# Two more pairs of gates as seven-product jobs, and the gated branch woven into the attention

## The chip, the cores and the metric

The kernel runs on one core of a Trainium2 chip. The metric is the device time of one execution in microseconds. The core has a matrix engine (TensorE, PE in the profile), a vector engine (VectorE, DVE), a scalar engine (ScalarE, ACT), GpSimd (POOL) and SyncE (SP), which here only issues DMAs. Each engine takes its instructions in the order in which they stand in its own list, and waits where an operand or a buffer is not ready.

## The reference

One decoder layer over 1024 tokens with 1024 channels, in float32. What matters here is its first half:

```python
xn = rms_norm(h, norm_mix_g)
sb_q, sb_k, sb_v, g_q, g_k, g_v, g_r, g_a, gate_sb, gate_gla = split(xn @ w_in)
o_sb = stick_breaking_attention(sb_q, sb_k, sb_v)       # 8 heads of 64, strictly causal
log_a = log_sigmoid(g_a @ w_alpha_up + b_alpha) / 16
o_gla = gla_chunked(g_q * 64 ** -0.5, g_k, g_v, log_a)  # 4 heads, gated linear attention
o_gla = o_gla * rsqrt(mean(o_gla ** 2) + eps) * gla_norm_g * silu(g_r)
y = sigmoid(gate_sb + b_gate[0]) * (o_sb @ w_branch_sb) + sigmoid(gate_gla + b_gate[1]) * (o_gla @ w_branch_gla)
h = h + y @ w_out
```

In the stick-breaking attention the weight of token s for token t is `sigmoid(z) * prod(sigmoid(-z))` over the tokens between them. A feed-forward part with a causal convolution and a last norm follow; the change doesn't touch them.

## The kernel before

Each large product is made of two-part numbers: `split` (line 119) makes a high part with a ScalarE cast and the rest with a VectorE subtraction, and `mac` (196) multiplies high by high, high by low and low by high. A matmul has 128 x 128 weights and up to 512 columns.

The stages, in the program's order:

1. Norm and turning of x, then the values of the attention (`value`, line 367) and of the gated branch. Beside the latter, `sums` makes four sums of the quarters of x (VectorE), and `differences` the difference of each value row from the one before (SP loads, one POOL subtraction on line 445, a POOL store to `dv_d`).
2. Jobs (`fast`): two columns of 128 of `w_in` are multiplied by x with seven quarter products in place of eight, 7 x 12 = 84 matmuls a job. `project_pairs` lists them: queries, keys, the gated branch's swish gates, and the first `N_GATES` = 4 of the 16 merge gates, 10 pairs in all. `decayed` runs beside them as `side`.
3. `attend`: 8 heads, 8 rows of 128 tokens, 288 blocks of 128 x 128. A piece of up to four blocks goes through scores (664), a sigmoid (666), a POOL select that sets what lies over the diagonal to 1 (668), a scan along the row that multiplies from the diagonal leftwards (671), transposes (678), `split`, and `gather` with the value differences (687). `gather` evicts the lower half with a bias (692), adds the upper half (116) and stores to `osb_d` (695). Up to six pieces or 12 blocks (`AHEAD`, `BLOCKS`) lie between the scan and the transposes.
4. `gates` computes the other 12 gates directly, 48 matmuls a gate, in steps of six matmuls of 512 columns. It is a generator: the attention takes one step of it for every `FILL` = 3.6 blocks, a few more at its start, and `BEFORE` = 4 follow it. These steps fill PE between the attention's short matmuls.
5. `gated` (states 781, scores 805, outputs 818 and 830, root mean square 842 to 847, transposes 853) comes behind, woven at two to three with `first_branch`, the product of the attention's output with `w_branch_sb`. This needs `osb_d` loaded back and split (955, 956).
6. The second branch, the output product, the feed-forward part.

Tiles come from pools: `t2` holds 11 of 128 x 512, `t4` 14 of twice that, `t8` 16 of four times; a tile is given out anew when its last reader is done. A scheduler puts the instructions of these generators in order for each engine.

Of the kernel before, what the change touches and what calls it, by code (L numbers as in the profile page):

```python
# [65 lines left out]
def block_kernel(ctx: ExitStack, tc: tile.TileContext, x, norm_mix_g, w_in, b_gate, w_alpha_up, b_alpha,  # L66
# [368 lines left out]
    def differences(i):  # L435

        a, b = t2(), t2()
        rows = slice(i * P, (i + 1) * P)
# [6 lines left out]
        nc.gpsimd.tensor_tensor(out=a, in0=a, in1=b, op=ALU.subtract)
# [211 lines left out]
    def weigh(t, e, i, b0, b1, right):  # L657
# [8 lines left out]
        nc.scalar.activation(ke[:, 0:w], z[:, 0:w], AF.Sigmoid, scale=-SBD ** -0.5)  # L666
        if right is None:
            nc.gpsimd.affine_select(out=ke[:, w - P:w], in_=ke[:, w - P:w], pattern=[[-1, P]],  # L668
                                    compare_op=ALU.is_gt, fill=1.0, base=0, channel_multiplier=1)
# [1 line left out]
        nc.vector.tensor_tensor_scan(out=kr, data0=kr, data1=zero.to_broadcast([P, w]),  # L671
                                     initial=1.0 if right is None else right[:, 0:1], op0=ALU.mult, op1=ALU.add)
# [8 lines left out]
    def gather(head, tp, ah, al):  # L681
# [7 lines left out]
        o = by(t2(), 2)  # L689
        for n in range(2):  # L690
            c = slice(n * P, (n + 1) * P)
            nc.scalar.activation(o[0:64, 1, c], po[64:128, c], AF.Identity,
                                 bias=vend[:, head * NT + 2 * tp + n:head * NT + 2 * tp + n + 1])
# [1 line left out]
        nc.sync.dma_start(osb_d[head * 64:(head + 1) * 64, tp * 2 * P:(tp + 1) * 2 * P], o[0:64, 0])
# [52 lines left out]
    owed = 0  # L748
    for w in attend():
        owed += w + EACH  # L750
        while owed >= FILL:
            owed -= FILL
            fill(gate_steps, 1)

# [6 lines left out]
    small = [by(t2(), 4) for _ in range(2)]  # L761
    state = [(v[:, 0], v[:, 1]) for v in small]

    gv, gla = [], []
    for p in range(2):
        rows = slice(p * P, (p + 1) * P)
        v, kt = by(t8(F32), 2), t4()
        nc.sync.dma_start(kt, kt_d[rows, :])
        v4 = by(t8(F32), 4)
        nc.sync.dma_start(v4, gv_d[p * HALF:(p + 1) * HALF, :].rearrange("(n p) c -> p n c", p=P))  # L770
        gv += [v4[:, n] for n in range(4)]
        nc.sync.dma_start(v[:, 0], qd_d[rows, :])
        nc.sync.dma_start(v[:, 1], ki_d[rows, :])
        gla.append((v[:, 0], v[:, 1], by(kt, NT), by(t4(), NT)))
# [103 lines left out]


# [69 lines left out]
    fill(gate_steps, BEFORE)  # L949
    ob = []  # L950
    for th in range(2):
        ob.append(quarter())
        for k in range(4):
            raw = t2()
            nc.sync.dma_start(raw, osb_d[k * P:(k + 1) * P, th * HALF:(th + 1) * HALF])
# [326 lines left out]
```

## Time and profile before

| | |
|---|---|
| median of 3 runs | 1410.92 us (1410.8 to 1413.48) |
| the profiled execution | 1412.8 us |
| its span | 1411.1 us |
| mean granted clock of TensorE | 0.994 |

The time is that of the whole execution, the span runs from the first to the last recorded instruction. In a view by stretches each row gives for one stretch the busy time of each engine with its number of instructions, then the granted TensorE clock as a share of full speed, and the DMA's share and rate. A chain of waits is read in order of time: each piece is what the next one waited for. Groups give the busy time, the mean of one instruction in ns, and the idle time of the engine before them. A matmul of float32 numbers that are not split stands there as two records.

### The profile page before, as it was taken

Reading aid. Unit: us, or ns where it says so; the run is one execution under the profiler, and the core shown is the slowest. Engines: PE = TensorE matmul, PEld = TensorE weight load, DVE = VectorE, ACT = ScalarE, POOL = GpSimd, SP = SyncE. Lnnn points to the kernel's source line nnn. Section 1 sums busy time; section 2 is a strip of 40 time slices with the busy share of each in tenths; the row PEclk is TensorE's granted clock in tenths of the full one; section 3 lists DMA queues with packets and bytes.
Section 4 is the critical chain, followed back from the end, with each engine's and each line's share of the span. In section 5 each row is a group of like instructions: output and inputs, shape, how many; then the busy total and the mean of one; then the engine's idle time right before and its main releaser. Section 6 shows DMA issues by size and latency. Waiting matters only on the chain.

```text
span 1411.1 us, 18434 instructions
## 1 busy us (share of the span) xinstructions
PE 1385.3 (98%) x6577; PEld 1145.4 (81%) x6577; DVE 1065.4 (76%) x1642; ACT 650.4 (46%) x1246; POOL 111.5 (8%) x198
## 2 busy tenths in 40 slices
PE   7999999999999999999999999999999999999997
PEld 6787888888888888878888788888888888888886
DVE  6398766767888875638446998998888977896765
ACT  6234444647766664543234543333333333454653
POOL 0040000001211110300000000100000000000000
PEclk9999999999999999999999999999999999999999
DMA  6365144276534346465324434564554437953332
GB/s 249 141 203 148 47 142 142 82 211 203 152 94 122 113 150 202 167 224 179 117 93 135 103 107 149 189 209 140 179 179 149 159 106 270 328 163 101 98 106 97
DMA packets 160188, 216.87 MB, mean 154 GB/s; under 512 B 10026, under 2 KB 103276, under 8 KB 159584
## 3 DMA queue, kind: packets, MB, share of 16 engines
q1 hardware_dynamic: 140848, 157.56, 36.5%
q0 software_dynamic: 11952, 43.58, 8.1%
q10 hardware_dynamic: 7296, 14.55, 2.8%
q8 instruction: 52, 0.85, 0.2%
q14 instruction: 40, 0.33, 0.1%
HBM read 155.75 MB, written 59.90 MB: 153 GB/s over the span
## 4 chain that ended last, share of the span: by engine, by line
PE 79%; issue 11%; DVE 6%; DMA 2%; ACT 1%; POOL 1%; POOLq 0%; ACTq 0%; DVEq 0%; SPq 0%
PE bank L196 46%; PE bank L1145 15%; PE bank L1012 5%; PE bank L367 3%; DVE t L110 3%; PE bank L687 2%; DVE t L116 2%; PE bank L664 2%; PE bank L678 2%; PE bank L320 1%; DMA gate_d<-t 1%; PE bank L427 1%; PE bank L818 1%; ACT t L119 0%; PE bank L781 0%
## 5 line engine op out<-in xcount | busy, mean ns | idle before, releaser
L196 PE MATMUL bank<-t,t 128*128 128x512 f32 x3648 | 870.6, 394 | 3.0 <-DVE t L110 2.6
L196 PEld LDWEIGHTS bank<-t,t 128*128 128x128 f32 x3648 | 682.7, 189 | 150.6 <-DVE t L110 3.8
L110 DVE TENSOR_TENSOR t<-t,t 128x512 fp32r<-128x512 f32 (+2 forms) x651 | 430.9, 696 | 82.6 <-ACT t L119 76.0
L119 ACT CAST t<-t 128x512 fp32r<-128x512 f32 x537 | 311.8, 620 | 321.5 <-DVE t L116 74.0
L116 DVE TENSOR_TENSOR t<-bank,t 128x512 f32<-128x512 f32 (+1 forms) x284 | 183.2, 655 | 119.9 <-PE bank L196 65.3
L1145 PE MATMUL bank<-t,t 128*128 128x512 f32 x924 | 209.6, 389 | 0.0
L1145 PEld LDWEIGHTS bank<-t,t 128*128 128x128 f32 x924 | 173.4, 188 | 36.0
L110 DVE TENSOR_TENSOR t<-t 128x512 f32<-128x512 f32 (+1 forms) x124 | 88.4, 721 | 5.6 <-DMA t<-in_w_ffn_in_dram 3.2
L367 PE MATMUL bank<-t,t 128*128 128x512 f32 x384 | 91.9, 398 | 0.0
L110 DVE TENSOR_TENSOR t<-bank,t 128x512 fp32r<-128x512 f32 (+4 forms) x128 | 72.2, 576 | 24.3 <-ACT t L119 23.9
L116 DVE TENSOR_TENSOR t<-t,t 128x512 f32<-128x512 f32 x107 | 76.8, 750 | 16.1 <-ACT t L487 15.4
L1012 PE MATMUL bank<-t,t 128*128 128x512 f32 x384 | 88.9, 391 | 0.0
L1043 ACT ACTIVATE t<-t,vcol 128x1024 f32<-128x1024 f32 x22 | 27.4, 1244 | 127.6 <-DVE t L116 124.0
L367 PEld LDWEIGHTS bank<-t,t 128*128 128x128 f32 x384 | 72.8, 192 | 15.6 <-DVE t L110 0.4
L1012 PEld LDWEIGHTS bank<-t,t 128*128 128x128 f32 x384 | 71.6, 188 | 14.7
L119 ACT CAST t<-bank 128x512 fp32r<-128x512 f32 (+3 forms) x124 | 61.6, 509 | 40.2 <-PE bank L320 19.7
L1045 DVE SCALAR_TENSOR_TENSOR t<-t,vcol,t 128x1023 f32<-128x1023 f32 (+1 forms) x44 | 56.3, 1279 | 14.1 <-ACT t L1043 13.9
L671 DVE TENSOR_TENSOR_SCAN t<-t,zero 128x128 f32<-128x128 f32 (+1 forms) x64 | 52.2, 823 | 16.0 <-POOL t L668 15.5
L664 PE MATMUL bank<-t,t 128*128 128x128 f32 (+3 forms) x192 | 55.5, 368 | 0.4 <-DVE t L110 0.4
L678 PE MATMUL bank<-ident,t 128*128 128x128 f32 x288 | 52.3, 274 | 0.8 <-DVE t L116 0.4
L668 POOL TENSOR_SCALAR_AFFINE_SELECT t<-t 128x128 f32<-128x128 f32 x64 | 33.3, 526 | 212.4 <-ACT t L666 199.2
L666 ACT ACTIVATE t<-bank 128x128 f32<-128x128 f32 (+3 forms) x96 | 45.7, 499 | 6.0 <-PE bank L664 4.3
(127 smaller groups left out, 773.6 us busy)
## 6 DMA issues: line engine op xcount, KB each, us to landing
t<-in_w_ffn_in_dram SPq DMA_DIRECT2D x50, 512.0 KB, 4.2
t<-in_w_in_dram SPq DMA_DIRECT2D x43, 512.0 KB, 5.3
act_d<-t POOLq DMA_DIRECT2D x22, 512.0 KB, 6.0
t<-in_w_ffn_out_dram SPq DMA_DIRECT2D x22, 512.0 KB, 7.5
wsum_d<-t POOLq DMA_DIRECT2D x22, 512.0 KB, 4.1
t<-act_d SPq DMA_DIRECT2D x22, 512.0 KB, 6.1
t<-wsum_d SPq DMA_DIRECT2D x44, 256.0 KB, 3.1
t<-sqk_d SPq DMA_DIRECT2D x40, 256.0 KB, 4.2
```

The costliest lines, as they stand in the source:

```text
L110: nc.vector.tensor_tensor(out=o, in0=a, in1=b, op=ALU.subtract)
L116: nc.vector.tensor_tensor(out=o, in0=a, in1=b, op=ALU.add)
L119: nc.scalar.copy(h, src)
L196: nc.tensor.matmul(pt, a[:, kk], b[:, kk], start=start and kk == 0 and m == 0, stop=stop and kk == k - 1 and m == 2)
L367: nc.tensor.matmul(pt, a[:, k % 4, t], b, start=k == 0 and m == 0, stop=k == NK - 1 and m == 2)
L664: nc.tensor.matmul(z[:, 0:w], q[:, a, e, ts_], kk[:, e, b0 * P:b1 * P], start=a == 0, stop=a == 1)
L666: nc.scalar.activation(ke[:, 0:w], z[:, 0:w], AF.Sigmoid, scale=-SBD ** -0.5)
L671: nc.vector.tensor_tensor_scan(out=kr, data0=kr, data1=zero.to_broadcast([P, w]), initial=1.0 if right is None else right[:, 0:1], op0=ALU ...
L678: nc.tensor.transpose(pt[:, b * P:(b + 1) * P], ke[:, b * P:(b + 1) * P], ident)
L1012: nc.tensor.matmul(pt, a[:, k % 4, t], b, start=(k == 0 and m == 0), stop=(k == NK - 1 and m == 2))
L1045: nc.vector.scalar_tensor_tensor(out=cv[:, i:], in0=av[:, :S - i], scalar=col(V_CW, (2 - i) * NF + f), in1=cv[:, i:], op0=ALU.mult, op1=AL ...
L1145: nc.tensor.matmul(pts[m][i], a[:, t], b, start=(k == 0 and x_ == 0), stop=(k == NH - 1 and x_ == 2))
```

## The change

`N_GATES` becomes 8: two more pairs of gates are jobs, 12 in all, and 8 gates are left to `gates`. `gates_and_gated` chains the remaining gate steps, the loads of the gated branch (`fetch_gated`) and the steps of `gated`, and the attention takes its filling from this chain; what is left of it behind the attention is woven with `first_branch`. `differences` leaves the stage of the sums, and is called from the loop over the jobs; its loads go from SP's queue to POOL's. The select is gone: a mask `above` that is made once enters the scan as second operand, with a maximum. `gather` stores both halves apart, and they are added behind the load of `osb_d`.

```diff
-N_GATES = 4
+N_GATES = 8
...
-        nc.sync.dma_start(b, sbv_d[rows, :])
+        nc.gpsimd.dma_start(b, sbv_d[rows, :])
...
     for i in range(NT):
-        differences(i)
         fill(xsums, 2)
         value(ws2, (i + 4) % NT, gv_d)
...
     for n, _ in enumerate(steps):
         if n > 0 and n % 2 == 0:
             fill(side, 1)
+        elif n // 2 < NT:
+            differences(n // 2)
...
+    above = t2()
+    nc.gpsimd.memset(above[:, P:], 0.0)
+    nc.gpsimd.memset(above[:, 0:P], 1.0)
+    nc.gpsimd.affine_select(out=above[:, 0:P], in_=above[:, 0:P], pattern=[[-1, P]], compare_op=ALU.is_ge, fill=0.0,
+                            base=P - 1, channel_multiplier=-1)
...
         if right is None:
-            nc.gpsimd.affine_select(out=ke[:, w - P:w], in_=ke[:, w - P:w], pattern=[[-1, P]],
-                                    compare_op=ALU.is_gt, fill=1.0, base=0, channel_multiplier=1)
-        kr = ke[:, 0:w][:, ::-1]
-        nc.vector.tensor_tensor_scan(out=kr, data0=kr, data1=zero.to_broadcast([P, w]),
-                                     initial=1.0 if right is None else right[:, 0:1], op0=ALU.mult, op1=ALU.add)
+            nc.vector.tensor_tensor_scan(out=kr, data0=kr, data1=above[:, 0:w], initial=1.0, op0=ALU.mult, op1=ALU.max)
+        else:
+            nc.vector.tensor_tensor_scan(out=kr, data0=kr, data1=zero.to_broadcast([P, w]), initial=right[:, 0:1],
+                                         op0=ALU.mult, op1=ALU.add)
...
-            nc.scalar.activation(o[0:64, 1, c], po[64:128, c], AF.Identity,
-                                 bias=vend[:, head * NT + 2 * tp + n:head * NT + 2 * tp + n + 1])
-        add(o[0:64, 0], po[0:64, 0:2 * P], o[0:64, 1])
-        nc.sync.dma_start(osb_d[head * 64:(head + 1) * 64, tp * 2 * P:(tp + 1) * 2 * P], o[0:64, 0])
+            nc.scalar.activation(o[:, c], po[:, c], AF.Identity, bias=vend[:, i:i + 1])
+        for n, r in enumerate(HALVES):
+            nc.sync.dma_start(osb_d[n * HALF + head * 64:n * HALF + (head + 1) * 64, tp * 2 * P:(tp + 1) * 2 * P], o[r])
...
+    def gates_and_gated():
+
+        yield from gate_steps
+        xq.clear()
+        fetch_gated()
+        yield
+        yield from gated()
+
+    filling = gates_and_gated()
+    owed = 0
+    for w in attend():
+        owed += w + EACH
+        while owed >= FILL:
+            owed -= FILL
+            fill(filling, 1)
...
-    fill(gate_steps, BEFORE)
+    fill(filling, BEFORE)
...
-            raw = t2()
-            nc.sync.dma_start(raw, osb_d[k * P:(k + 1) * P, th * HALF:(th + 1) * HALF])
-            split(*(a[:, k] for a in ob[th]), raw)
+            halves = t2(), t2()
+            for n, v in enumerate(halves):
+                nc.sync.dma_start(v, osb_d[n * HALF + k * P:n * HALF + (k + 1) * P, th * HALF:(th + 1) * HALF])
+            add(halves[0], *halves)
+            split(*(a[:, k] for a in ob[th]), halves[0])
     first_branch = branch(0, ob, w_branch_sb)
     fill(first_branch, 1)
-    fill(gate_steps, 128)
-    xq.clear()
-    og = [quarter() for _ in range(2)]
     n = 0
-    for _ in gated():
+    for _ in filling:
```

How this moves instructions is seen best at three places. In the rows below a name gives the tile that is written, behind the arrow the tiles that are read, and then the shape; the line is that of the kernel whose rows they are.

On PE in the last quarter of the attention, before: transposes (L678), scores (L664), and the matmuls of a direct gate (L196) between them.

```order
L678 MATMUL bank_5144<-ident,t_928_5030 128x128 x3
L664 MATMUL bank_5150<-t_794_4362,t_843_4627 128x384 x2
L196 MATMUL bank_5115<-t_485_2831,t_899_4915 128x512
L196 MATMUL bank_5115<-t_484_2830,t_899_4915 128x512 x2
L196 MATMUL bank_5115<-t_485_2831,t_899_4915 128x512
L196 MATMUL bank_5115<-t_484_2830,t_899_4915 128x512
L678 MATMUL bank_5171<-ident,t_934_5070 128x128 x4
L664 MATMUL bank_5178<-t_794_4362,t_843_4627 128x512 x2
L678 MATMUL bank_5190<-ident,t_937_5087 128x128 x4
L664 MATMUL bank_5197<-t_794_4362,t_843_4627 128x512 x2
```

And in the changed kernel, where L686 are the transposes, L672 the scores, L806 and L769 outputs and states of the gated branch:

```order
L686 MATMUL bank_5083<-ident,t_949_4966 128x128
L686 MATMUL bank_5087<-ident,t_951_4972 128x128 x4
L672 MATMUL bank_5094<-t_844_4523,t_904_4782 128x256 x2
L686 MATMUL bank_5100<-ident,t_955_4990 128x128 x2
L672 MATMUL bank_5105<-t_844_4523,t_904_4782 128x512 x2
L806 MATMUL bank_5111<-t_886_4728,t_964_5030 128x128 x4
L686 MATMUL bank_5121<-ident,t_961_5017 128x128 x4
L672 MATMUL bank_5128<-t_844_4523,t_904_4782 128x384 x2
L769 MATMUL bank_5134<-t_890_4736,t_885_4726 128x256
```

The gate's matmuls of 512 columns have gone from between the attention's, and one state or one output of four short matmuls stands in the place of each step.

On PE at the end of the attention, before, from the last gather (L687) on; the matmuls behind it are of two direct gates:

```order
L687 MATMUL bank_5322<-t_946_5125,t_526_3021 128x128
L196 MATMUL bank_5230<-t_55_321,t_953_5168 128x512 x2
L196 MATMUL bank_5230<-t_56_322,t_953_5168 128x512
L196 MATMUL bank_5230<-t_55_321,t_953_5168 128x512
L196 MATMUL bank_5373<-t_484_2830,t_966_5243 128x512
L196 MATMUL bank_5373<-t_485_2831,t_966_5243 128x512
L196 MATMUL bank_5373<-t_484_2830,t_966_5243 128x512 x2
L196 MATMUL bank_5373<-t_485_2831,t_966_5243 128x512
L196 MATMUL bank_5373<-t_484_2830,t_966_5243 128x512 x2
```

And now, from the last scores of an output pair (L793) behind the last gather on; L841 are its transposes:

```order
L793 MATMUL bank_5486<-t_884_4725 128x128
L841 MATMUL bank_5501<-ident,t_1050_5422 128x128 x4
L806 MATMUL bank_5509<-t_890_4736,t_1061_5495 128x128 x4
L841 MATMUL bank_5515<-ident,t_1053_5436 128x128 x4
L806 MATMUL bank_5510<-t_890_4736,t_1062_5498 128x128 x4
L818 MATMUL bank_5509<-t_887_4732,t_884_4725 128x128
L818 MATMUL bank_5510<-t_887_4732,t_884_4725 128x128
```

Behind the last gather there were 41 matmuls of gates ahead of the first one of `first_branch`; now there are 15 scores, 8 transposes and 16 output matmuls of the gated branch, and eight scores of the next pair.

On ACT, one output pair of the gated branch, before (squares L842, root L843, scaling L847), among casts of the branch's weights:

```order
L842 ACTIVATE t_1049_5659,ss_1050_5660<-bank_5613 128x128 x4
L842 ACTIVATE t_1052_5673,ss_1053_5674<-bank_5614 128x128
L843 ACT_TABLE_LOAD
L843 ACTIVATE ss_1050_5660<-ss_1050_5660,eps 128x4
L842 ACTIVATE t_1052_5673,ss_1053_5674<-bank_5614 128x128 x2
L847 ACTIVATE t_1049_5659<-bank_5613,ss_1050_5660 128x128 x4
L842 ACTIVATE t_1052_5673,ss_1053_5674<-bank_5614 128x128
L119 CAST t_1132_6149<-t_1131_6147 128x512
L843 ACTIVATE ss_1053_5674<-ss_1053_5674,eps 128x4
```

And now the first of them, which stands in the attention (squares L830, root L831, scaling L835, the attention's sigmoid L674):

```order
L830 ACTIVATE t_1007_5197,ss_1008_5198<-bank_5111 128x128 x4
L830 ACTIVATE t_1010_5211,ss_1011_5212<-bank_5112 128x128
L831 ACT_TABLE_LOAD
L831 ACTIVATE ss_1008_5198<-ss_1008_5198,eps 128x4
L830 ACTIVATE t_1010_5211,ss_1011_5212<-bank_5112 128x128 x2
L835 ACTIVATE t_1007_5197<-bank_5111,ss_1008_5198 128x128 x4
L830 ACTIVATE t_1010_5211,ss_1011_5212<-bank_5112 128x128
L119 CAST t_966_5036<-bank_5224 128x4x128
L831 ACTIVATE ss_1011_5212<-ss_1011_5212,eps 128x4
L674 ACT_TABLE_LOAD
L674 ACTIVATE t_1014_5234<-bank_5231 128x512
L835 ACTIVATE t_1010_5211<-bank_5112,ss_1011_5212 128x128 x4
```

The pair now has the attention's sigmoid behind it, and a second table load ahead of that one.

More of the change, by code (lines that the diff above doesn't have):

```diff
@@ L159, in block_kernel @@
     gate_d, ga_d = dram("gate_d", 2 * D, S), dram("ga_d", 2 * RANK, S)
-    osb_d = dram("osb_d", SBH * SBD, S)
+    osb_d = dram("osb_d", 2 * SBH * SBD, S)
     x21_d = dram("x21_d", 2 * P, 2 * D)
@@ L438, in differences @@
         rows = slice(i * P, (i + 1) * P)
-        nc.sync.dma_start(b, sbv_d[rows, :])
+        nc.gpsimd.dma_start(b, sbv_d[rows, :])
         if i == 0:
             nc.gpsimd.memset(a[0:1], 0.0)
-            nc.sync.dma_start(a[1:P], sbv_d[0:P - 1, :])
+            nc.gpsimd.dma_start(a[1:P], sbv_d[0:P - 1, :])
         else:
-            nc.sync.dma_start(a, sbv_d[i * P - 1:(i + 1) * P - 1, :])
+            nc.gpsimd.dma_start(a, sbv_d[i * P - 1:(i + 1) * P - 1, :])
         nc.gpsimd.tensor_tensor(out=a, in0=a, in1=b, op=ALU.subtract)
@@ L635, in block_kernel @@
     vt = []
-    vend = t2()[0:SBD, 0:SBH * NT]
+    vend = t2()[:, 0:SBH * NT]
+    above = t2()
[3 more added lines that the diff above has]
+                            base=P - 1, channel_multiplier=-1)
     def last_values():
@@ L644, in last_values @@
             nc.tensor.transpose(pt[0:SBD, h * NT:(h + 1) * NT], raw[0:NT, h * SBD:(h + 1) * SBD], ident[0:NT, 0:NT])
-        nc.vector.tensor_copy(vend, pt[0:SBD, 0:SBH * NT])
+        nc.gpsimd.memset(vend[SBD:P], 0.0)
+        nc.vector.tensor_copy(vend[0:SBD], pt[0:SBD, 0:SBH * NT])
     def value_blocks(n):
@@ L747, in block_kernel @@
     last_values()
[L748 to L753, printed above, removed]
     def after(b, a):
@@ L759, in after @@
                           reason="bank order")
[L761 to L774, printed above, removed]
+    state, gv, gla, og = [], [], [], []
     def states(p, n0, n1):
@@ L877, in gated, with fetch_gated @@
                     yield
+    def fetch_gated():
+        small = [by(t2(), 4) for _ in range(2)]
+        state.extend((v[:, 0], v[:, 1]) for v in small)
+        for p in range(2):
+            rows = slice(p * P, (p + 1) * P)
+            v, kt = by(t8(F32), 2), t4()
+            nc.sync.dma_start(kt, kt_d[rows, :])
+            v4 = by(t8(F32), 4)
+            nc.sync.dma_start(v4, gv_d[p * HALF:(p + 1) * HALF, :].rearrange("(n p) c -> p n c", p=P))
+            gv.extend(v4[:, n] for n in range(4))
+            nc.sync.dma_start(v[:, 0], qd_d[rows, :])
+            nc.sync.dma_start(v[:, 1], ki_d[rows, :])
+            gla.append((v[:, 0], v[:, 1], by(kt, NT), by(t4(), NT)))
+        og.extend(quarter() for _ in range(2))
+    def gates_and_gated():
[11 more added lines that the diff above has]
+            fill(filling, 1)
     yq, yb, hq, hs1 = {}, {}, {}, {}
```

4 lines of the change are left out of this document (3 added, 1 removed).

## The prediction

> **What bounds the kernel now.** I read the page's busy shares first, then busy time by stretches, then the chain of waits, and only then single instructions.
>
> ```profile
> span 1411.1 us, 18434 instructions
> PE 1385.3 (98%) x6577; PEld 1145.4 (81%) x6577; DVE 1065.4 (76%) x1642; ACT 650.4 (46%) x1246; POOL 111.5 (8%) x198
> ```
>
> TensorE is busy 98% of the span, so a gain must take matmuls away or fill one of the few places where PE waits. The stretches show where these are, and how near the second engine is.
>
> ```profile
> 105.00:140.00 35.00, 32.89 (x134) 25.30 (x133) 29.92 (x47) 13.97 (x25) 2.53 (x3) 0.95 0.50 149
> 455.00:490.00 35.00, 35.00 (x204) 30.17 (x203) 30.43 (x43) 21.51 (x47) 6.33 (x10) 1.00 0.39 114
> 560.00:595.00 35.00, 35.00 (x222) 28.80 (x221) 23.99 (x51) 20.50 (x70) 10.50 (x18) 1.00 0.61 205
> 595.00:630.00 35.00, 32.31 (x184) 25.90 (x183) 15.08 (x27) 16.96 (x68) 2.37 (x4) 0.90 0.58 197
> 665.00:700.00 35.00, 35.00 (x157) 28.96 (x156) 19.13 (x31) 7.69 (x13) 0.00 (x0) 1.00 0.22 68
> ```
>
> Columns after the length: PE, PEld, DVE, ACT, POOL, granted clock, DMA. Two stretches lose time: 105 to 140 (2.11 us idle, and a clock of 0.95 costs about 1.75) and 595 to 630 (2.69 idle, clock 0.90, about 3.5). In the attention (455 to 490) PE is full, but VectorE already works 30.4 of 35 us. That nearness decides this change: the attention has matmuls of the gates woven in, which cost PE much and VectorE little.
>
> **Matmuls removed.** Four gates leave the direct form (96 matmuls a pair) for jobs of 84, so 2 x 12 = 24 matmuls of 512 columns go.
>
> ```profile
> 795.95 396.51 PE bank L196 x1748
> ```
>
> One takes 396.51 / 1748 = 0.2268 us back to back: 24 x 0.2268 = **-5.4 us**, all of it on PE, which bounds there. The jobs add VectorE and ScalarE work, but in their stretch VectorE has room; I price that at nothing.
>
> **The differences leave the sums.** At 70 to 117 VectorE makes the sums of x, and the chain of waits runs through it until PE gets its operand:
>
> ```profile
> 115.88 0.61 DVE t L110
> 116.54 3.73 PE bank L196 x10
> ```
>
> ```profile
> 74.83 2.38 DVE L116 TENSOR_TENSOR t<-t,t 128x512 f32<-128x512 f32 x2
> 83.22 1.28 DVE L116 TENSOR_TENSOR t<-t,t 128x512 f32<-128x512 f32 x2
> ```
>
> ```profile
> 75.14 1.52 POOL L445 TENSOR_TENSOR t<-t,t 128x512 f32<-128x512 f32 x1 [20.36 <-DMA t<-sbv_d]
> ```
>
> A pair of adds takes 1.28 us alone and 2.38 us where a POOL subtraction runs beside it: 1.1 us. Eight such subtractions are in that stretch; 8 x 1.1 = 8.8 us is more than PE waits for. They move to the jobs, nine of them now since block 0 is done twice, with their loads on POOL's queue instead of SP's. What they hold up there is POOL's own stores behind them, and VectorE, which has room.
>
> ```profile
> 112.00:117.00 5.00, 3.23 (x15) 2.37 (x14) 5.00 (x9) 2.34 (x5) 0.20 (x1) 1.00 0.56 170
> 117.00:122.00 5.00, 4.66 (x14) 3.10 (x13) 4.37 (x8) 2.35 (x6) 0.00 (x0) 0.66 0.14 52
> ```
>
> PE loses 1.77 + 0.34 us of idle and 0.34 x 5 = 1.70 us of clock: **-3.8 us**, bounds 0 and -3.8; I take the whole, since 8.8 covers the 2.1 idle four times. [...]
>
> **What the attention loses and gains throughout.** A select on POOL goes from every first scan, an addition after every gather, and 32 more stores of the same size go to SP, since the two halves of the output are stored apart.
>
> ```profile
> L668 POOL TENSOR_SCALAR_AFFINE_SELECT t<-t 128x128 f32<-128x128 f32 x64 | 33.3, 526 | 212.4 <-ACT t L666 199.2
> ```
>
> ```profile
> L116 DVE TENSOR_TENSOR t<-bank,t 64x256 f32<-64x256 f32 x32 | 12.9, 402 | 15.1 <-ACT t L692 15.1
> ```
>
> ```profile
> 545.63 0.45 SPq L695 DMA_DIRECT2D osb_d<-t  x1
> ```
>
> 33.3 us of POOL and 12.9 of VectorE lie beside a PE that is full there (455 to 490), and 32 x 0.45 = 14.4 us of issue spread over some 200 us of a queue that mostly waits: nothing, while direct gates are the cover. Where that cover ends, the next part counts.
>
> **The last stretch of attention.** Direct gates are used up after 1 + 6 + 58 steps; 58 steps at 3.6 blocks are some 209 of the 288 blocks of the attention. For the rest (87 transposed blocks by the order) gated steps are woven in. They cost VectorE and ScalarE more and PE less than a gate's step. Up to the last matmuls of L695 the order gives for DVE 16 first scans (four of each width), 8 second ones, 28 subtractions from PSUM (15, 5, 4, 4 by width), one of 1024, two of 512, 24 state updates, and a few small ones.
>
> ```profile
> L671 DVE TENSOR_TENSOR_SCAN t<-t,t,zero 128x512 f32<-128x512 f32 x32 | 41.0, 1282 | 7.1 <-ACT t L666 6.2
> L110 DVE TENSOR_TENSOR t<-bank,t 128x512 fp32r<-128x512 f32 x48 | 31.9, 669 | 1.5 <-ACT t L119 1.4
> L671 DVE TENSOR_TENSOR_SCAN t<-t,zero 128x512 f32<-128x512 f32 x16 | 19.4, 1214 | 8.5 <-POOL t L668 8.5
> L671 DVE TENSOR_TENSOR_SCAN t<-t,zero 128x384 f32<-128x384 f32 x16 | 15.1, 946 | 1.8 <-POOL t L668 1.8
> L671 DVE TENSOR_TENSOR_SCAN t<-t,zero 128x256 f32<-128x256 f32 x15 | 10.6, 704 | 3.6 <-POOL t L668 3.2 <-DMA t<-sqk_d 0.4
> L671 DVE TENSOR_TENSOR_SCAN t<-t,zero 128x128 f32<-128x128 f32 x15 | 6.4, 428 | 0.3 <-POOL t L668 0.2
> ```
>
> ```profile
> L790 DVE SCALAR_TENSOR_TENSOR t<-t,eend,bank 64x128 f32<-64x128 f32 x24 | 8.3, 345 | 1.3 <-PE bank L781 0.7
> ```
>
> Scans 4 x (1.214 + 0.946 + 0.704 + 0.428) + 8 x 1.282 = 23.4; subtractions about 18 (15 x 0.669 the largest part); states 24 x 0.345 = 8.3; the rest near 3: 52.7 us. Instructions that follow each other overlap a little:
>
> ```profile
> 540.39 1.89 DVE L110 TENSOR_TENSOR t<-bank,t 128x512 fp32r<-128x512 f32 x3 [0.20 <-ACT t L119]
> ```
>
> Three take 1.89, not 2.01, so 0.06 less at each joint; over 77 instructions VectorE needs 48 us at least. The new mask operand of the scan changes its sources, not its length; I cost it at nothing; 0.1 us more or less in each of the 24 scans would be 2.4 us. PE in the same rows:
>
> ```profile
> 542.70 1.74 PE bank L687 x15
> 551.09 0.43 PE bank L781 x2
> 566.75 1.09 PE bank L805 x16
> 571.69 0.89 PE bank L818 x8
> 577.11 0.87 PE bank L830 x12
> 584.49 0.44 PE bank L853 x4
> ```
>
> (an f32 matmul is two records): 114 gathers 12.2 (0.116, the narrow ones half), 87 + 8 transposes at 0.11 10.5, 48 scores by width 8.2, 13 states at 0.43 5.6, and 45 more at 0.14 to 0.22 7.6: 44 us. VectorE exceeds PE by 4 us at the least. On top come ScalarE's bursts: an output pair of the gated branch is 8 squares with their reads, 8 scalings, two roots, and now two table loads, since the roots stand between the attention's sigmoids.
>
> ```profile
> 611.62 1.38 ACT t L842 x10
> ```
>
> ```profile
> L847 ACT ACTIVATE t<-bank,ss 128x128 f32<-128x128 f32 x32 | 9.5, 422 | 0.0
> L843 ACT ACT_TABLE_LOAD x1 | 1.3, 1283 | 0.0
> ```
>
> 8 x 0.276 + 8 x 0.30 + 2 x 1.28 + 0.7 = 7.8 us, in which the sigmoids and casts queued behind get little. Up to 12 blocks lie ready (0.55 us of DVE each), so I give the first burst 2.5 us of VectorE's time and the second, with nothing behind it, 5. So 48 + 7.5 = 55.5 against 44: **+11.5**, bounds +4 and 52.7 + 15.6 - 44 = +24.
>
> **Behind the attention.** The first branch waits for the attention's output: eviction, store, load, split.
>
> ```profile
> 544.27 6.82 PE L196 MATMUL bank<-t,t 128*128 128x512 f32 x29
> 546.81 5.22 SPq L955 DMA_DIRECT2D t<-osb_d  x8
> 551.17 3.35 PE L196 MATMUL bank<-t,t 128*128 128x512 f32 x13
> ```
>
> The last gather ended at 544.4; the branch's first matmul is the 13th of the last row, 551.17 + 12 x 0.227 = 553.9. These 9.5 us were full of gates. Now 15 + 8 + 8 + 8 short matmuls stand there, 5.8 us by the rows above, and the loads are 16 at 5.22 / 8 = 0.65 us of issue, with an addition before each split; behind them on SP stand the loads of gates that the branch multiplies by. Idle is 3.7 at the least of this chain, 5.6 with two more loads issued ahead; I take **+4.5**, with 0 as the low end if loads overtake. An idle PE also loses clock (row at 117 to 122): one window of that size is **+1.7**, bounds 0 and 5. For the gated tail (595 to 630) I change nothing: its last transposes still stand behind a cast that waits for VectorE.
>
> **Sum.** -5.4 - 3.8 + 11.5 + 4.5 + 1.7 = +8.5. The profiled execution took 1412.8 us (span 1411.1), 1.9 over the median 1410.92; the terms are differences, so I add them to the median: **1419**.
>
> **The rivals.** *The engines run side by side.* The pieces ready ahead carry VectorE over both bursts and loads overtake: +4, +3 and no clock lost, -9.2: 1409. It decides once stretch and chain cost under 9.2 together. For it: gates and gated steps already mix without loss at 560 to 610. Against it: VectorE is over PE by sum alone. *The same, and the gated tail goes too* (its 6.2 us, having more branch behind it): 1403. *VectorE is held by POOL.* The gated steps bring their POOL work into the stretch that VectorE now bounds:
>
> ```profile
> L792 POOL TENSOR_SCALAR t<-t,emid 128x128 f32<-128x128 f32 x14 | 8.2, 588 | 44.8 <-DVE t L788 30.8 <-DVE t L790 13.3 <-ACT t L809 0.6
> L810 POOL TENSOR_SCALAR_AFFINE_SELECT t<-t 128x512 f32<-128x512 f32 x8 | 5.1, 637 | 18.9 <-ACT t L809 10.4 <-DMA t<-gr_d 8.4
> ```
>
> 12 x 0.588 + 4 x 0.637 = 9.6 us; if each delays a scan as the subtractions did the adds, 1429; with the upper ends of stretch, chain and clock instead (-9.2 + 24 + 5.6 + 5) 1436. Against it: the 64 selects of before lay beside scans whose mean stayed at 1.21 to 1.28 us. [...]
>
> **How the numbers follow.** Forecast (1413 to 1428) 0.52; side by side 0.22, half of it within 0.2% (which is about what a measurement can tell); tail gone too 0.08; POOL or worse 0.18. Faster is 0.08 + 0.11 = 0.19; same 0.11 + 0.05 of the forecast's lower edge = 0.16; slower 0.65. The range 1403 to 1436 leaves out half of the 1403 case and some of the worst, under 0.15.
>
> **What would show it.** Right: no idle and clock 1.00 at 112 to 122; VectorE near full in the last quarter of the attention while PE falls to about 80%; an idle gap and a half clock ahead of the first branch. Wrong: PE full through the end of the attention; selects or scalings on POOL that stretch scans; a wait in the jobs for POOL's loads.

## The result and the profile after

The changed kernel takes 1431.02 us (median of 5 runs, 1429.61 to 1433.14) against 1413.05 (5 runs, 1410.8 to 1414.13) of the kernel before: a ratio of 1.0138, with a 95% interval of 1.0126 to 1.0149 (the two medians alone give 1.0127). It is slower by some 18 us where 8.5 were forecast, and 3 us above the upper end of the forecast's range, 1428. The profiled execution has a span of 1429.3, 18.2 over that of before.

The page of the changed kernel, its span and the shares of busy time:

```profile
span 1429.3 us, 18288 instructions
PE 1383.9 (97%) x6553; PEld 1144.1 (80%) x6553; DVE 1071.6 (75%) x1646; ACT 652.6 (46%) x1252; POOL 89.8 (6%) x159
```

The 24 matmuls are gone (6577 to 6553), and the span is longer all the same, so PE waits more. The stretches of the changed kernel show where; the columns are those of the prediction (length, PE, PEld, DVE, ACT, POOL, granted clock, DMA).

```profile
112.00:117.00 5.00, 5.00 (x24) 4.13 (x23) 4.96 (x8) 2.58 (x5) 1.84 (x2) 1.00 0.28 105
117.00:122.00 5.00, 5.00 (x24) 4.14 (x23) 4.44 (x7) 2.50 (x6) 1.75 (x4) 1.00 0.53 148
349.70:404.70 55.00, 54.57 (x301) 45.81 (x300) 44.34 (x65) 41.65 (x86) 0.00 (x0) 1.00 0.68 201
455.00:490.00 35.00, 35.00 (x215) 30.55 (x214) 25.03 (x38) 22.72 (x52) 0.00 (x0) 1.00 0.91 266
511.40:577.40 66.00, 54.26 (x380) 46.00 (x378) 51.56 (x90) 46.58 (x138) 10.47 (x17) 0.96 0.19 57
518.00:545.00 27.00, 23.17 (x161) 18.95 (x162) 26.37 (x50) 15.55 (x42) 7.21 (x12) 1.00 0.15 36
545.00:577.00 32.00, 24.09 (x170) 20.50 (x170) 20.10 (x33) 24.71 (x81) 3.26 (x5) 0.93 0.23 74
577.00:604.00 27.00, 18.05 (x107) 14.70 (x107) 17.37 (x29) 16.40 (x48) 2.97 (x4) 0.77 0.78 255
591.30:604.00 12.70, 10.53 (x34) 8.08 (x35) 9.61 (x16) 5.19 (x9) 1.73 (x2) 0.66 0.84 268
604.00:640.00 36.00, 33.10 (x162) 26.85 (x161) 17.86 (x30) 11.52 (x38) 0.00 (x0) 1.00 0.76 251
```

The sums (112 to 122) have lost their idle and their slow clock. The attention's first scores come at 349.7, where in the kernel before they came at 316.2. In the first 55 us from there PE idles 0.43 us; the kernel before idled 1.71:

```profile
316.20:371.20 55.00, 53.29 (x287) 43.92 (x285) 43.48 (x66) 40.10 (x83) 8.79 (x16) 1.00 0.62 185
```

PE stays nearly full as long as direct gates last (161.27 of the 161.7 us from 349.7 to 511.4). Then come three different things. From 518 to 545 VectorE is full, 26.37 of 27 us, and PE is not. From 545 to 577 VectorE is no longer full, 20.10 of 32, and PE still isn't. And from 577 to 604 PE idles 8.95 us and runs at a clock of 0.77.

What happens at 545 to 577 shows in the timeline: here the second of two bursts of ScalarE and the instructions of PE and VectorE that wait for it. Columns: start, time, engine, line, operation, and in brackets the idle time before it with what ended it.

```profile
566.60 1.09 PE L686 MATMUL bank<-ident,t 128*128 128x128 f32 x8
566.70 0.28 ACT L830 ACTIVATE t<-bank 128x128 f32<-128x128 f32 x1 [0.80 <-PE bank L818]
...
568.12 1.28 ACT L831 ACT_TABLE_LOAD   x1
...
570.12 1.14 ACT L835 ACTIVATE t<-bank,ss 128x128 f32<-128x128 f32 x4
...
571.37 0.62 ACT L119 CAST t<-bank 128x512 fp32r<-128x512 f32 x1
...
572.02 0.69 DVE L110 TENSOR_TENSOR t<-bank,t 128x512 fp32r<-128x512 f32 x1 [2.10 <-ACT t L119]
...
572.72 0.58 PE L695 MATMUL bank<-t,t 128*128 128x256 f32 x1 [5.02 <-ACT t L119]
...
573.95 3.46 PE L695 MATMUL bank<-t,t 128*128 128x256 f32 x15
```

The last transposes stand ready at 567.7. The cast that follows them stands behind the normalisation of two heads of the gated branch (squares 830, a table load and root 831, scaling 835), so VectorE's subtraction comes late and PE's last gather waits 5 us. The last 15 gather matmuls then run at half clock (0.50 granted at 572.7 to 577.4): 3.46 us, where at 0.116 each they take 1.74. The same comes once more behind the attention:

```profile
581.51 15.55 SPq L976 DMA_DIRECT2D t<-osb_d  x16
...
584.66 0.27 ACT L830 ACTIVATE t<-bank 128x128 f32<-128x128 f32 x1
...
589.40 1.15 ACT L835 ACTIVATE t<-bank,ss 128x128 f32<-128x128 f32 x4
...
590.61 0.62 ACT L119 CAST t<-t 128x512 fp32r<-128x512 f32 x1
591.28 0.80 PE L196 MATMUL bank<-t,t 128*128 128x512 f32 x1 [6.36 <-ACT t L119]
```

The first matmul of the first branch starts at 591.28, 13.9 us after the last gather (573.95 + 3.46 = 577.4). Two things stand in this time: a third burst (584.66 to 590.5), and 16 loads that take 15.55 us from the first issue to the last. Most of the 15.55 is waiting of the queue, since one issue takes 0.34 us by the median (the three numbers are shortest, median and longest, in ns):

```profile
L976 SPq DMA_DIRECT2D t<-osb_d x16: 319/340/867, 581.5 to 596.7; - x16
```

What the queue waits for was not tried apart; tiles that the late casts give free late are a candidate. More is lost behind the branch's first matmul: at 591.3 to 604 PE idles 2.17 us, and the clock is 0.66.

### The profile page after: what moved, and what is told of

Read it like the earlier page. It is cut to its first block, busy times and chain, and to the rows that moved or that the text cites. A ratio compares the mean times of both kernels' runs of the same rounds, so it can differ in the third digit from the quotient of the medians.

```text
span 1429.3 us, 18288 instructions
## 1 busy us (share of the span) xinstructions
PE 1383.9 (97%) x6553; PEld 1144.1 (80%) x6553; DVE 1071.6 (75%) x1646; ACT 652.6 (46%) x1252; POOL 89.8 (6%) x159
## 4 chain that ended last, share of the span: by engine, by line
PE 55%; DVE 3%; ACT 2%; DMA 1%; issue 1%; POOL 0%; SPq 0%; DVEq 0%; ACTq 0%; POOLq 0%
PE bank L196 34%; PE bank L1164 15%; PE bank L1031 5%; DVE t L110 2%; DMA t<-osb_d 1%; DVE t L116 1%; ACT t L830 0%; PE bank L695 0%; PE bank L806 0%; ACT t L119 0%; ACT t L835 0%; DVE t L679 0%; DVE t L677 0%; PE bank L320 0%; PE bank L818 0%
## 5 line engine op out<-in xcount | busy, mean ns | idle before, releaser
L196 PE MATMUL bank<-t,t 128*128 128x512 f32 x3624 | 849.9, 392 | 7.2 <-ACT t L119 6.4
L196 PEld LDWEIGHTS bank<-t,t 128*128 128x128 f32 x3624 | 678.7, 188 | 153.0 <-ACT t L119 7.1
L110 DVE TENSOR_TENSOR t<-t,t 128x512 fp32r<-128x512 f32 (+2 forms) x661 | 436.6, 695 | 82.8 <-ACT t L119 75.8
L116 DVE TENSOR_TENSOR t<-bank,t 128x512 f32<-128x512 f32 x266 | 179.6, 686 | 111.8 <-PE bank L196 72.9
L1164 PE MATMUL bank<-t,t 128*128 128x512 f32 x924 | 209.6, 389 | 0.0
L1164 PEld LDWEIGHTS bank<-t,t 128*128 128x128 f32 x924 | 173.4, 188 | 36.0
L110 DVE TENSOR_TENSOR t<-t 128x512 f32<-128x512 f32 (+1 forms) x128 | 92.3, 729 | 10.0 <-ACT t L601 6.4
L367 PE MATMUL bank<-t,t 128*128 128x512 f32 x384 | 90.6, 394 | 0.0
L1031 PE MATMUL bank<-t,t 128*128 128x512 f32 x384 | 88.9, 391 | 0.0
L367 PEld LDWEIGHTS bank<-t,t 128*128 128x128 f32 x384 | 71.8, 189 | 15.4 <-DVE t L110 0.4
L1031 PEld LDWEIGHTS bank<-t,t 128*128 128x128 f32 x384 | 71.6, 188 | 14.7
L1064 DVE SCALAR_TENSOR_TENSOR t<-t,vcol,t 128x1023 f32<-128x1023 f32 (+1 forms) x44 | 56.3, 1280 | 14.1 <-ACT t L1062 13.9
L677 DVE TENSOR_TENSOR_SCAN t<-t,t 128x128 f32<-128x128 f32 (+1 forms) x64 | 51.8, 816 | 15.5 <-ACT t L674 15.3
L695 PE MATMUL bank<-t,t 128*128 128x256 f32 (+1 forms) x320 | 48.7, 289 | 8.3 <-ACT t L119 5.0
L672 PE MATMUL bank<-t,t 128*128 128x128 f32 (+3 forms) x192 | 55.1, 370 | 0.9 <-DVE t L778 0.6
L695 PEld LDWEIGHTS bank<-t,t 128*128 128x128 f32 x320 | 44.9, 197 | 11.5 <-ACT t L119 5.3
L686 PE MATMUL bank<-ident,t 128*128 128x128 f32 x288 | 52.1, 276 | 1.0 <-ACT t L835 0.7
```

Of the source, the lines that this page charges most:

```text
L110: nc.vector.tensor_tensor(out=o, in0=a, in1=b, op=ALU.subtract)
L116: nc.vector.tensor_tensor(out=o, in0=a, in1=b, op=ALU.add)
L196: nc.tensor.matmul(pt, a[:, kk], b[:, kk], start=start and kk == 0 and m == 0, stop=stop and kk == k - 1 and m == 2)
L367: nc.tensor.matmul(pt, a[:, k % 4, t], b, start=k == 0 and m == 0, stop=k == NK - 1 and m == 2)
L672: nc.tensor.matmul(z[:, 0:w], q[:, a, e, ts_], kk[:, e, b0 * P:b1 * P], start=a == 0, stop=a == 1)
L677: nc.vector.tensor_tensor_scan(out=kr, data0=kr, data1=above[:, 0:w], initial=1.0, op0=ALU.mult, op1=ALU.max)
```

## The experiments

The theory: VectorE's own work bounds the last stretch, ScalarE's bursts stretch it further, and burst and loads together make the chain behind it. The rivals are named in each expectation. All ratios are to the kernel before, with their 95% intervals.

### Steps that last through the attention

```diff
-FILL = 3.6
+FILL = 5.8
-BEFORE = 4
+BEFORE = 8
```

> The changed kernel with 5.8 blocks instead of 3.6 between two steps of the filling and 8 steps instead of 4 kept for behind the attention: the direct gates then last through the attention, and all of the gated branch lies behind it, with the first branch. Theory A (the loss sits where gated steps fill the attention, and in the bare chain behind it): both go, and the gains that the trace shows before and at the start of the attention stay (5.4 of matmuls, 4.3 in the sums, 3.9 at 325 to 380): 1413 - 13.6 = 1399, to 1403 if the longer reload is not wholly covered; VectorE below 95% everywhere in the attention. Rival B (the attention has too little matmul work per block for VectorE as soon as a step comes only every 5.8 blocks, whatever the step is): VectorE full and PE at about 90% over all of the attention, 1410 to 1420. Rival C (the loss is in the new store and load alone): 1425 or more.

1416.86 us, 1.0037 (1.0024 to 1.005). 14 us of the loss go, so most of it hangs on where the direct gates end. The time lies in B's range, yet not for B's reason alone; what remains is in two places of this run:

```profile
380.00:410.00 30.00, 27.13 (x160) 21.78 (x159) 27.85 (x38) 24.17 (x52) 0.00 (x0) 1.00 0.71 178
440.00:480.00 40.00, 40.00 (x258) 35.30 (x257) 36.85 (x52) 28.91 (x68) 0.00 (x0) 1.00 0.50 131
548.00:566.00 18.00, 11.36 (x38) 7.31 (x37) 11.96 (x22) 6.46 (x11) 3.29 (x1) 0.91 0.93 316
```

Where the values are split as well (380 to 410) VectorE is at 93% and PE loses 2.9 us, which is B's mechanism; behind that VectorE is at 92% and PE is full, so B doesn't hold over all of the attention. The other place is the chain behind the attention, where PE waits for the operands of the first branch.

### The old store and load of the output

```diff
-        for n, r in enumerate(HALVES):
-            nc.sync.dma_start(osb_d[n * HALF + head * 64:n * HALF + (head + 1) * 64, tp * 2 * P:(tp + 1) * 2 * P], o[r])
+        add(o[0:64, 0], po[0:64, 0:2 * P], o[0:64, 1])
+        nc.sync.dma_start(osb_d[head * 64:(head + 1) * 64, tp * 2 * P:(tp + 1) * 2 * P], o[0:64, 0])
...
-            for n, v in enumerate(halves):
-                nc.sync.dma_start(v, osb_d[n * HALF + k * P:n * HALF + (k + 1) * P, th * HALF:(th + 1) * HALF])
-            add(halves[0], *halves)
+            nc.sync.dma_start(raw, osb_d[k * P:(k + 1) * P, th * HALF:(th + 1) * HALF])
```

> The changed kernel with the attention's output stored as before (the two halves added ahead of one store; 8 loads instead of 16 and no addition behind them). Theory A (the doubled stores and loads make the chain behind the attention longer, 13.9 us against 9.5): 1431 - 5 = 1426, first matmul of the first branch some 5 us earlier. Rival B (that chain is held by ScalarE's casts and the wait for the last output pair): 1430 to 1431. Rival C (the addition that VectorE gets back, 32 x 0.40 us, lies in a stretch that VectorE bounds): no better than 1431, up to 1435.

1431.87 us, 1.0145 (1.0129 to 1.0162): no better than the changed kernel. The loads are half as many, and the first branch still waits:

```profile
577.07 3.44 PE L695 MATMUL bank<-t,t 128*128 128x256 f32 x15
...
584.43 10.65 SPq L975 DMA_DIRECT2D t<-osb_d  x8
...
593.98 0.80 PE L196 MATMUL bank<-t,t 128*128 128x512 f32 x1 [4.31 <-ACT t L119]
```

13.5 us, and ScalarE's casts end them. So the loads alone do not make this chain. Rival C holds in part as well: with the additions back on VectorE, the stretch from the last direct gate to the last gather takes 68.4 us in place of 66.0, and VectorE is busy for 54.52 us of it in place of 51.56:

```profile
512.10:580.50 68.40, 54.82 (x380) 46.06 (x378) 54.52 (x100) 47.55 (x138) 10.47 (x17) 0.95 0.15 45
```

In the kernel with 5.8 blocks, where no burst stands behind the attention, the same edit was made:

> The changed kernel with both edits of the two runs before: 5.8 blocks between two steps of the filling with 8 steps kept, and the old store and load of the attention's output (8 loads instead of 16, no addition behind them). In the run with 5.8 blocks alone PE lost 9.9 us at 548 to 566, waiting for operands of the first branch behind 16 loads and 8 additions. Theory A (there, with direct gates as cover and no bursts on ScalarE, the doubled loads are what is late): most of it goes, 1417 - 7 = 1410. Rival B (as at the end of the changed kernel, where the old store changed nothing): 1416 to 1417. Both keep the 6 us lost at 380 to 415, where VectorE has the splits of the values to make and steps come rarely.

1411.85 us, 0.9998 (0.999 to 1.0007): 5.0 under the run with 5.8 blocks alone, as theory A has it, if less than the 7 it named. So the doubled loads, with the additions behind them, do cost where no burst holds the chain.

### The gates alone

```diff
-N_GATES = 4
+N_GATES = 8
```

This is the only edit to the kernel before.

> The kernel before with nothing but eight pairs of gates as jobs instead of four: the direct gates are used up about 87 blocks before the attention ends, and nothing fills the rest; the gated branch stays behind it. Theory A (VectorE alone bounds the rest of the attention: first and second scans 23.4 and subtractions about 18, less overlaps, some 39 us, against some 31 of PE): -5.4 + 8, and the chain behind it wholly bare, + 9.5, and 1.7 of clock: 1413 + 13.8 = 1427; PE at 75 to 80% and VectorE at 95% or more at the end of the attention. Rival B (the rest of the attention runs at PE's pace when ScalarE has no bursts of the gated branch): -5.4 + 9.5 + 1.7 = 1419, VectorE below 95%.

1422.62 us, 1.0081 (1.0066 to 1.0095). Three stretches of it:

```profile
112.00:117.00 5.00, 3.18 (x14) 2.33 (x13) 5.00 (x10) 2.00 (x4) 0.00 (x0) 1.00 0.60 167
352.80:407.80 55.00, 53.79 (x291) 44.70 (x289) 44.61 (x68) 40.99 (x85) 9.85 (x16) 1.00 0.62 190
518.00:558.00 40.00, 31.50 (x218) 26.02 (x216) 38.77 (x62) 27.80 (x72) 7.66 (x16) 1.00 0.13 37
```

VectorE is at 97% and PE at 79% in the bare rest of the attention, which takes theory A's side. Counted in matmuls at the prices of the prediction, PE has about 29 us of work in the 44 from its last direct gate to its last gather, so this rest alone costs 14 us without any gated step, 6 more than A gave it. The time still came out 4.4 under A's 1427, since the bare chain is short:

```profile
558.15 2.00 PE L687 MATMUL bank<-t,t 128*128 128x256 f32 x15 [0.45 <-DVE t L110]
559.98 0.65 PE L781 MATMUL bank<-t,t 128*128 128x256 f32 x2
564.91 0.50 PE L196 MATMUL bank<-t,t 128*128 128x512 f32 x1 [4.28 <-ACT t L119]
```

From the end of the last gather to the first branch it takes 4.8 us, not 9.5.

### The differences alone

```diff
     for i in range(NT):
-        differences(i)
...
+        elif n // 2 < NT:
+            differences(n // 2)
```

Their two loads go to POOL's queue, as in the change.

> The kernel before with nothing but the move of the differences of the values: out of the sums and into the jobs, their loads on POOL's queue. Theory A (they held VectorE's adds, for which PE waited): 1413 - 4 = 1409, no idle and full clock at 112 to 122. Rival B (what PE gains there is lost again in the jobs): 1413. Rival C (the 3.9 us at the start of the attention come from this move too): 1405.

1409.47 us, 0.9987 (0.9978 to 0.9997). In its trace the idle and the low clock at 112 to 122 are gone, as in the changed kernel (PE 10.00 of 10 us, clock 1.00); at 325 to 380 it loses about 2 us more than before (a clock of 0.97 there), so the gain is nearer 2 than 4.

### The mask alone

```diff
-            nc.gpsimd.affine_select(out=ke[:, w - P:w], in_=ke[:, w - P:w], pattern=[[-1, P]],
-                                    compare_op=ALU.is_gt, fill=1.0, base=0, channel_multiplier=1)
...
+            nc.vector.tensor_tensor_scan(out=kr, data0=kr, data1=above[:, 0:w], initial=1.0, op0=ALU.mult, op1=ALU.max)
```

> The kernel before with nothing but the mask as the scan's second operand in place of the select on POOL. Theory A (the select lies beside a PE that is full; the mask does not lengthen the scan): 1411.5 within 1. Rival B (the 3.9 us that the changed kernel gains at 325 to 380 come from the select's going): 1407.6. Rival C (the mask lengthens each of the 64 first scans by 0.1 us or more): nothing where direct gates last, so 1411 to 1413, but a longer mean in the trace.

1411.62 us, 1.0003 (0.9994 to 1.0011): nothing, as predicted. A group of its trace, the first scans of 512 columns, keeps the mean of before:

```profile
L675 DVE TENSOR_TENSOR_SCAN t<-t,t 128x512 f32<-128x512 f32 x16 | 19.4, 1214 | 7.5 <-ACT t L672 7.5
```

PE still idles 2.05 us at 325 to 380 in this run, where the attention starts as in the kernel before (316.4). So the smaller loss at the start of the attention in the changed kernel does not come from the select.

### Without the normalisation, and without the state

The core of the first edit:

```diff
-            for n in range(4):
-                nc.scalar.activation(ot[:, w], po[:, w], AF.Square, accum_out=ss[:, n:n + 1])
-            nc.scalar.activation(ss, ss, AF.Sqrt, bias=eps, scale=1.0 / GV)
-            nc.vector.reciprocal(ss, ss)
-            for n in range(4):
-                nc.scalar.activation(ot[:, w], po[:, w], AF.Copy, scale=ss[:, n:n + 1])
+            nc.scalar.copy(ot, po)
```

> The changed kernel without the normalisation of the gated branch's output: squares, root, reciprocal and scaling are left out, and one copy of 512 columns on ScalarE takes their place for each head. Theory A (the normalisation, about 6 us of ScalarE for two heads together, keeps the casts of the attention and of its output waiting, in three places: 546 to 555, 567 to 574, 585 to 591): VectorE no longer idles 14 us in the last stretch of the attention, the chain behind it falls from 13.9 to about 9.5 us: 1431 - 10 - 6 = 1415, with up to 2 more in the gated tail. Rival B (VectorE's own work and the number of tiles hold the stretch; ScalarE merely shows idle time of others): only the three table loads go, 1428 or more.

1419.7 us, 1.0058 (1.0045 to 1.007): 11.3 under the changed kernel, most of what theory A said and far from B's 3. The rest of the difference to A is the chain, which stayed. Its stretches and its last rows:

```profile
513.00:545.00 32.00, 28.80 (x202) 24.44 (x200) 29.58 (x54) 21.18 (x56) 6.84 (x11) 1.00 0.13 36
545.00:571.00 26.00, 22.17 (x185) 19.48 (x184) 20.55 (x33) 14.63 (x32) 3.97 (x6) 1.00 0.31 98
```

```profile
568.98 2.00 PE L695 MATMUL bank<-t,t 128*128 128x256 f32 x15
...
574.54 11.70 SPq L968 DMA_DIRECT2D t<-osb_d  x11
...
584.02 1.95 PE L196 MATMUL bank<-t,t 128*128 128x512 f32 x3 [6.48 <-ACT t L119]
```

VectorE does the work of the second part (20 us in both kernels) in 26 us in place of 32, at full clock, and the last gathers take 2.00 us. From the last direct gate to the last gather it is 57.6 us (513.4 to 571.0) in place of 66.0, so the normalisation costs 8.4 here. VectorE isn't full even without them: it is busy for 50.1 of the 57.6. The chain is still 13.0 us (584.02 - 570.98). With the old store added to this:

> The changed kernel without the normalisation of the gated branch's output and with the old store and load of the attention's output (8 loads). Without the normalisation alone the time was 1419.7 and the first matmul of the first branch still came 13.3 us after the last gather; with the old store alone it came 13.9 us after it. Theory A (either of the two is enough to hold that chain: the burst on ScalarE ahead of the casts, or the 16 loads and 8 additions): with both gone it falls to about 9.5 us, 1420 - 4 = 1416. Rival B (a third cause holds it, such as loads or tiles of the gated branch): 13 us again, 1419 to 1420.

1415.15 us, 1.0027 (1.0016 to 1.0038): theory A. The chain falls to 10.0 us:

```profile
571.90 1.99 PE L695 MATMUL bank<-t,t 128*128 128x256 f32 x15
...
577.32 7.65 SPq L967 DMA_DIRECT2D t<-osb_d  x8
...
583.87 0.51 PE L196 MATMUL bank<-t,t 128*128 128x512 f32 x1 [2.50 <-ACT t L119]
```

Taking away the loads alone left the chain at 13.5 us, and taking away the bursts left it at 13.0: either is enough to hold it at 13 to 14 us, and only both together shorten it. What holds the 10.0 that are left was not tried; with eight gates alone it is 4.8.

The 4.5 us that this run gains on the one before do not come from an earlier first matmul: it starts at 583.87 in place of 584.02, since the last gather ends 2.9 us later, with the additions back on VectorE. They come from behind it. Without the normalisation alone, and then with the old store as well:

```profile
584.00:604.00 20.00, 18.10 (x85) 13.67 (x86) 17.84 (x27) 9.66 (x17) 1.38 (x2) 0.80 0.86 300
584.00:604.00 20.00, 19.75 (x110) 15.86 (x111) 16.17 (x26) 10.39 (x19) 1.64 (x2) 1.00 0.93 325
```

PE idles 1.9 us in the first row and 0.25 in the second, and in the second the clock doesn't fall.

The core of the other edit:

```diff
-                    nc.vector.scalar_tensor_tensor(out=new[r], in0=st[r], scalar=eend[p][r, n:n + 1], in1=src,
-                                                   op0=ALU.mult, op1=ALU.add)
```

> The changed kernel without the 24 additions by which VectorE carries the state of the gated branch on (the first of each row is kept and scaled again; PE's matmuls and POOL's scalings stay). They take 8.3 us of VectorE, nearly all at 520 to 545, where it works 26.4 of 27 us. Theory A (VectorE bounds that half of the stretch): 1431 - 7 = 1424. Rival B (what PE waits for there is ScalarE or the number of tiles, and VectorE is full only by chance): 1430 to 1431.

1427.69 us, 1.011 (1.0095 to 1.0124): 3.3 under the changed kernel, half of A's 7. PE's time from the last direct gate to the last gather falls by some 4.9 us (66.0 to 61.1), not by the 8.3 that VectorE is spared. VectorE does bound there, but where it is relieved, something else is late after a few us. What that is was not tried apart.

### What could be kept

Six gates more or less as jobs, and the pace of the steps set so that direct gates last:

```diff
-N_GATES = 8
+N_GATES = 6
-FILL = 3.6
+FILL = 4.6
-BEFORE = 4
+BEFORE = 8
```

with the old store:

> The changed kernel with three pairs of gates as jobs instead of four, so 10 direct gates, a step every 4.6 blocks, 8 steps kept for behind the attention, and the old store and load of its output; the gated branch then lies wholly with the first branch. Theory A (the loss comes from direct gates that run out, and the gains are the matmuls, 2.7 with this number, 4.3 in the sums and up to 3.9 at the start of the attention): 1412 - 7 to 1412 - 11: 1401 to 1405. Rival B (fewer steps between blocks make VectorE late anyway, as with 5.8): 1407 to 1410.

1414.61 us, 1.0019 (1.0011 to 1.0028): neither A nor B. The steps last, but behind the attention the gated branch's first state waits 4.36 us for its values, which in this order are loaded after the attention's output:

```profile
557.05 0.67 PE L769 MATMUL bank<-t,t 128*128 128x256 f32 x2 [4.36 <-DMA t<-gv_d]
```

So the next run is made from the kernel before, which has these loads earlier:

> The kernel before with the differences moved into the jobs and three pairs of gates as jobs, a step every 4.6 blocks, 8 steps kept; store, mask and the place of the gated branch (with its loads ahead of those of the attention's output) as before. Theory A (what this change can gain is its matmuls and the sums, as long as direct gates last and the gated branch's loads are early): 1411.5 - 2.7 - 4.3 = 1404.5, up to 1409 if the start of the attention gives back as much as where the differences alone were moved. Rival B (a step every 4.6 blocks already makes VectorE late at the start of the attention): 1409 to 1412.

1409.0 us, 0.9981 (0.9973 to 0.999): the best, and a little faster than the kernel before, but 4.5 above A's first number, where A and B meet. The differences alone gave 0.9987 (0.9978 to 0.9997), so the runs do not show that the two gates more add anything to that. At 380 to 400 it loses 1.5 us in 20:

```profile
380.00:400.00 20.00, 18.51 (x119) 15.85 (x118) 17.02 (x26) 14.05 (x32) 5.54 (x9) 1.00 0.54 152
```

So more steps were given to that place:

> The same with a step every 3.6 blocks in the first 72 blocks, where VectorE also splits the values, and every 5.1 behind them. Theory A (VectorE is late only where the values are split): 2 to 4 us under the run with 4.6 throughout. Rival B (5.1 is too rare behind it): the same or up to 3 above.

1412.54 us, 1.0006 (0.9997 to 1.0016): rival B, at 3.5 above the run with 4.6. PE is not full at 455 to 490 here (32.55 of 35, clock 0.95), where with 4.6 it is.

## Why the prediction had the sign and half of the size

The measured sizes below are counted in both traces as a stretch's length less its matmuls at the back-to-back prices of the prediction, and the attention is taken from its first scores on in both; behind the attention, idle time and lost clock give nearly the same numbers.

| term | predicted | measured |
|---|---|---|
| 24 matmuls | -5.4 | -5.4 |
| differences leave the sums | -3.8 | -4.3 |
| attention, up to the last direct gate | 0 | -2.1 |
| last stretch of the attention | +11.5 | +19.0 |
| behind the attention, with clock | +6.2 | +14.5 |
| gated tail | 0 | -3.2 |
| sum | +8.5 | +18.5 (spans: +18.2) |

**Matmuls and sums** are right. The differences alone show the same in the sums (no idle and clock 1.00 at 112 to 122), so this gain comes from their move; that kernel gives part of it back at the attention's start.

**What I cost at nothing:** the mask is nothing, shown by its own run. The attention up to its last direct gate loses 6.5 us by the count, where before its first 164 us lost 8.6; most of the difference lies at its start, where the rows above have 0.43 us of idle in place of 1.71. With eight gates alone it is 1.21, so the gates make a part of it at most; what makes the rest stays open. (The 3.9 us at 325 to 380 that some expectations name compares different work: in the changed kernel the first 25 of these 55 us are still jobs.) In the gated tail PE idles as before, 2.90 us at 604 to 640 where 2.69 were at 595 to 630, but the clock stays at 1.00. It did so in the run with the mask alone too, so this 3.2 can't be put down to the change:

```profile
595.00:630.00 35.00, 32.30 (x195) 26.19 (x195) 15.86 (x28) 17.07 (x69) 2.48 (x4) 1.00 0.64 217
```

**The last stretch** is where the sum failed most. That VectorE exceeds PE here is right, and PE's work is as predicted: 44.4 of 66 us, 21.6 over; the last 64 us of the attention before held 2.6 counted alike, so 19.0 is the change. The step that failed is the one from VectorE's work to the length: "VectorE needs 48 us at least" was taken as the time of the stretch without the bursts. The run without the normalisation shows that time, 57.6 us, 9.6 over. VectorE's own work is 50.1 there, and it stands still for the other 7.5, mostly waiting for ScalarE, for casts (119, 4.0 us) and sigmoids (674, 3.8). So an engine at 87% of the stretch did not run without gaps, and PE, which waits for it in order, lost them as well. Why these casts and sigmoids are late was not tried apart.

The term of the bursts came out near its size, 66.0 - 57.6 = 8.4 where 7.5 were taken; the split into 2.5 and 5 was not measured. The rows at 566 to 577 show how the second one acts: one cast is late, and the subtraction, the last gather and then the clock follow. The gates alone show that PE loses 14 us in the rest of the attention without any gated step. Here the gated steps were no filling. They hold about 15 us of PE's work (44 less the 29 of the bare rest), and lengthened the stretch by 22 (66 less 44).

**Behind the attention** the step "chain 9.5 us, cover 5.8" failed. 9.5 was read from the kernel before, where gates filled the time, and it is not the chain's own length: with eight gates alone it is 4.8 us, and with bursts or doubled loads 13 to 14. I had not put the third burst into this place at all. With 5.7 us of cover, 8.2 us are lost ahead of the branch's first matmul, where I took 4.5; the rest is lost behind it. The clock, put at the loss of the one row at 117 to 122, was 0.77 over 27 us, 6.2 us in place of 1.7. Idle 8.95 and clock 6.2 make 15.1, less the 0.6 that the same stretch lost before. (The 5.6 beside the 4.5 doesn't follow from its row: two more loads at 0.65 on 3.7 make 5.0.)

**The rivals.** Nothing ran side by side, so 1409 is out. POOL held VectorE, but little: in the last stretch the first scans have nearly the means of before (1210, 969, 683 and 412 ns by width, where 1214, 946, 703 and 428 were), and the nine second scans 1359 ns in place of 1282, 0.7 us together of the 9.6 that this rival gave:

```profile
L679 DVE TENSOR_TENSOR_SCAN t<-t,t,zero 128x512 f32<-128x512 f32 x9 | 12.2, 1359 | 4.1 <-ACT t L674 4.0
```

The 1429 that it named is near the result by chance. Of what would show the forecast right, full PE at 112 to 122 came. VectorE near full came in the first part only (26.37 of 27 us, with PE at 86%); over 511.4 to 577.4 VectorE is at 78% and PE at 82%. The idle gap ahead of the first branch came, with a low clock mostly beside it: 0.50 in the last gathers, and 0.66 at 591.3 to 604. Of the signs of wrong, one came in small, the scans that selects stretch.

## What to carry to other kernels

A filling is chosen by the engine that is second in the place it fills, not by PE: here the bare rest of the attention left VectorE almost no room (97% busy with eight gates alone), and a filling that needs VectorE and ScalarE lengthened the stretch by 22 us with 15 us of its own matmuls. The busy time of the engine that bounds a stretch is a lower bound of its length: VectorE, with 50.1 us of work, took 57.6 even without bursts. A burst has to be priced in every place where it falls, with what queues behind it in order and the clock that falls then (here 5.02 us of wait ahead of the last gathers, and 0.50 in them). And the length of a hidden chain is not the time that its cover took; it has to be bounded from both sides until a run shows it bare (here 4.8 us where 9.5 were taken).
